# Feed-forward of a streaming encoder: weights of two projections prepared once for both token sets, the third projection accumulated whole in PSUM

## The chip, the cores and the metric

The kernel runs on one core of a Trainium2 chip. The metric is device time in microseconds (us), the lower the better. Five engines work side by side, each through a list of instructions in a fixed order: PE (matrix products; its weight loads, PEld, overlap them), DVE and POOL (elementwise work; DVE reads PSUM too), ACT (copies, casts, activation functions; reads PSUM too) and SP, which here only issues DMA transfers. An instruction waits until what it needs is there, and all behind it on its engine wait with it. PSUM, where PE writes, has eight banks of 128 partitions x 512 numbers of 32 bits.

## The reference, cut to what matters

One encoder layer runs over 1088 tokens: 1024 of a prompt and 64 of a second group, all with the same weights. Projections, sparse attention, pooling and cross-attention come first; the change touches only what follows the merge. `x` is 1088 x 1024, `w_out` 1024 x 1024, `w_gate` and `w_up` 1024 x 2816, `w_down` 2816 x 1024, all in 32-bit floats:

```python
x = x + mixed @ w_out
h = x * rsqrt(mean(x * x, axis=-1) + 1e-6) * g_ffn
y = x + (silu(h @ w_gate) * (h @ w_up)) @ w_down
```

## The kernel before, in words

Activations lie transposed, features on partitions, tokens along the free dimension. The tokens are cut in two sets, `SETS = [(0, 512), (512, 576)]`.

**Three passes.** PE works on rounded numbers (type fp32r). Each operand is therefore split into a rounded part `hi` (a cast) and the rest `lo = x - hi` (a subtraction on DVE, `lo_of`, L86), and a product is three matmuls: hi*hi, hi*lo, lo*hi (`matmul3`, L120). `wblock` fetches 512 KB of weights by a DMA and splits them: the cast (`round_hi`) goes in turn to ACT (L94) and POOL (L96), the rest to DVE (L86).

**Projection by w_out** (`out_proj`, L1003 on). For each set and each of eight output blocks `f`: a `wblock`, 24 matmuls for each 512 or 288 tokens, a DVE addition into the resident `y` (L1014), a square on ACT (L1019), a sum of squares on POOL (L1020). From the sums `norm_stat` and `norm_rows` make the factor of each token, `rb`.

**Feed-forward.** The 22 blocks of 128 hidden features are taken as eleven pairs `p` (block `p` and block `p + 11`). A pair's product h @ w is seen as a 2 x 2 block product: two halves of the 1024 features, two halves of a set's tokens, two hidden blocks. It is done with seven products of sums of blocks in place of eight plain ones (Strassen's scheme). On the token side the sums are made once a set: `block_sums` (L1051 on) multiplies `y` by the norm (L1068), forms sums (L1076), casts (L1078) and subtracts (L86), for four feature blocks `k`. On the weight side `pair_product` (L1090 on) does it for each pair and set: two 512 KB loads, five sums of 128x512 (L1107, on DVE and POOL), seven casts on ACT (L1112), seven rests on DVE (`al`), 12 matmuls a product, copies of the first four results (L1119) and the additions that put the four quadrants together (L1121 to L1133, on POOL and DVE). `hidden` calls it for `w_gate` and `w_up`, applies Silu, multiplies, and splits the result `u` in hi and lo.

**Product with w_down** (`down`, L1153 on). A pair's `u` is multiplied by its rows of `w_down` in eight units, each a few matmuls and an addition into `y` (L1168). The units of a pair are run between the products of the next pair (`units`), so each output block is added to `y` eleven times.

The loops go over set 0 with pairs 0 to 10, then set 1 with pairs 0 to 10; the sums of set 1 are made in the last pair of set 0, from buffers of their own (`tg`, `st`). A scheduler sets the order of instructions on each engine from the program's order and its own estimate of durations; buffers rotate (`bufs=`), and a tile waits until the earlier user of its memory is done. All transfers named here go through SP's one list, in order.

Of the kernel before, what the change touches and what calls it, by code (L numbers as in the profile page):

```python
# [45 lines left out]
def encoder_step(ctx: ExitStack, tc: tile.TileContext, a: dict, o: list):  # L46
# [42 lines left out]
    third = [None]  # L89

    def round_hi(hi, src):
        turn[0] += 1
        if turn[0] % 2 and third[0]:
            A.copy(hi, src)  # L94
        else:
            G.tensor_scalar(hi, src, 1.0, 1.0, op0=OP.mult, op1=OP.mult)  # L96
# [873 lines left out]
    for k in range(KT):  # L970
        SP.dma_start(y[:, k], a["x_t"][k])
# [31 lines left out]
    def out_proj(i, between={}):  # L1003
        t0, n = SETS[i]
        sq = yp.tile([128, 576], F32, name="sq", tag="sq", bufs=1)
        for f in range(KT):
# [3 lines left out]
            for c0, cn in ([(t0, n)] if n <= 512 else halves(i)):  # L1010
# [40 lines left out]
    def block_sums(i, rb):  # L1051
        t0, n = SETS[i]
        h = n // 2
        hi, lo = [[hp.tile([128, 4, 288], F32R, name=f"{nm}{q}", tag=f"{nm}{q}", bufs=1) for q in range(7)]
                  for nm in ("hi", "lo")]
        for k in range(4):
            if i:
                hb = fu.tile([128, 2, 576], F32, name="tg", tag="tg", bufs=2)
                hb = [hb[:, e] for e in range(2)]
                sums = fu.tile([128, 4, 288], F32, name="st", tag="st", bufs=2)  # L1060
                sums = [sums[:, e, :h] for e in range(4)]
            else:
# [136 lines left out]
    while units:  # L1199
        units.pop(0)()  # L1200
# [65 lines left out]
```

## Time and profile before

| what | us |
|---|---|
| median of three runs (1804.94 to 1807.34) | 1806.07 |
| the profiled execution, its own time | 1805.8 |
| its span, first to last instruction | 1803.9 |
| first matmul of the projection by `w_out` | 925.2 |
| first matmul of the feed-forward | 1032.3 |
| last matmul begins | 1800.8 |

The page gives, for each engine, busy time, its share of the span and the number of instructions. A view by stretches ("windows") gives for a stretch of the span: its length, the busy time of PE, PEld, DVE, ACT and POOL each with the number of instructions in parentheses, the mean clock granted to PE (1.00 is full), the share of time that the 16 DMA engines were busy, and GB/s. A view by tiles gives for a group of instructions min/median/max of their durations in ns, and the start of the first and the last. A line of the timeline gives start, duration, engine, line, operation, output tile <- input tiles, form, and in brackets the idle time before it with what ended it. Matmuls are pipelined: one's recorded duration is longer than its distance to the next, so what PE really needs for one is read from the distances of starts.

### The profile page before, as it was taken

What the parts mean: (1) busy time and instruction counts of PE and PEld (TensorE: products, weight loads), DVE (VectorE), ACT (ScalarE), POOL (GpSimd) and SP (SyncE); (2) the same over time, 40 slices, a digit from 0 to 9 for tenths busy, and PEclk for the clock granted to TensorE, in tenths of its full rate; (3) what the DMA queues carried; (4) which work ended last, traced back from release to release, by engine and by line L of the source; (5) the groups of instructions that cost most, each with busy time, mean ns of one, the idle gap of its engine ahead of it and who ended that gap; (6) DMA issues with size and microseconds to landing.
All of it is one profiled execution on the core that took longest, in us unless ns stands there. A gap on an engine that the chain in (4) does not pass through costs nothing.

```text
span 1803.9 us, 32261 instructions
## 1 busy us (share of the span) xinstructions
PE 1731.5 (96%) x11762; PEld 1648.2 (91%) x11762; DVE 1441.2 (80%) x2779; ACT 854.4 (47%) x2013; POOL 812.7 (45%) x784
## 2 busy tenths in 40 slices
PE   6999999999999998999999899999997899999999
PEld 6999999999999998877899889899996799999999
DVE  6667999998953445889764899898899999898896
ACT  4456677726423443588422353443443434344442
POOL 4111323243531225764114665666658665555543
PEclk9999999999999999999999899999998899999999
DMA  7122441134355236721532223332322332222322
GB/s 227 60 66 83 159 137 53 57 121 131 104 165 170 86 104 235 218 90 40 220 119 84 82 88 100 103 109 82 109 91 82 105 106 91 86 95 81 106 74 73
DMA packets 123598, 198.24 MB, mean 110 GB/s; under 512 B 21031, under 2 KB 91807, under 8 KB 123438
## 3 DMA queue, kind: packets, MB, share of 16 engines
q1 hardware_dynamic: 123438, 196.16, 34.0%
q8 instruction: 93, 1.52, 0.3%
q14 instruction: 67, 0.55, 0.1%
HBM read 158.47 MB, written 37.65 MB: 109 GB/s over the span
## 4 chain that ended last, share of the span: by engine, by line
PE 58%; DVE 7%; issue 3%; POOL 2%; ACT 2%; DMA 1%; SPq 0%; DVEq 0%; ACTq 0%; POOLq 0%
PE mm L120 45%; PE fl L120 8%; PE acc L921 1%; DVE lo L86 1%; PE tr L891 1%; DVE al L86 1%; PE mm L914 1%; DVE wlo L86 1%; DMA gt<-side_m 0%; POOL ws L1107 0%; ACT pr L897 0%; PE mm L603 0%; DVE pr L895 0%; DVE ws L1107 0%; ACT ah L1112 0%
## 5 line engine op out<-in xcount | busy, mean ns | idle before, releaser
L120 PE MATMUL mm<-hi,ah 128*128 128x256 f32 (+1 forms) x1232 | 358.4, 291 | 9.9 <-ACT hi L1078 6.1
L120 PE MATMUL mm<-hi,al 128*128 128x256 f32 (+1 forms) x1232 | 358.4, 292 | 7.6 <-DVE al L86 7.6
L120 PE MATMUL mm<-lo,ah 128*128 128x256 f32 (+1 forms) x1232 | 358.9, 291 | 5.0 <-DVE lo L86 5.0
L86 DVE TENSOR_TENSOR al<-ws,ah 128x512 fp32r<-128x512 f32 x220 | 218.7, 1006 | 53.8 <-ACT ah L1112 51.5
L120 PE MATMUL mm<-u,whi 128*128 128x288 f32 (+1 forms) x1056 | 258.1, 330 | 0.7 <-DVE u L86 0.7
L1112 ACT CAST ah<-ws 128x512 fp32r<-128x512 f32 x220 | 135.4, 619 | 248.5 <-POOL ws L1107 142.0
L120 PEld LDWEIGHTS mm<-hi,ah 128*128 128x128 f32 x1232 | 234.9, 191 | 17.2 <-ACT hi L1078 8.3
L120 PEld LDWEIGHTS mm<-hi,al 128*128 128x128 f32 x1232 | 233.6, 190 | 11.9 <-DVE al L86 11.2
L120 PEld LDWEIGHTS mm<-lo,ah 128*128 128x128 f32 x1232 | 234.2, 190 | 10.9 <-DVE lo L86 6.5
L120 PE MATMUL fl<-hh,whi 128*128 128x362 f32 (+1 forms) x576 | 190.2, 331 | 1.0 <-ACT hh L133 1.0
L120 PE MATMUL fl<-hl,whi 128*128 128x362 f32 (+1 forms) x576 | 191.0, 332 | 0.0
L120 PE MATMUL fl<-hh,wlo 128*128 128x362 f32 (+1 forms) x576 | 189.8, 330 | 0.0
L120 PEld LDWEIGHTS mm<-u,whi 128*128 128x128 f32 x1056 | 175.2, 189 | 9.3 <-DVE u L86 1.1
L120 PE MATMUL mm<-u,wlo 128*128 128x288 f32 (+1 forms) x528 | 174.1, 330 | 0.0
L1107 POOL TENSOR_TENSOR ws<-raw 128x512 f32<-128x512 f32 x66 | 88.4, 1350 | 116.8 <-DVE al L86 116.8
L1168 DVE TENSOR_TENSOR y<-mm,y 128x288 f32<-128x288 f32 (+1 forms) x264 | 135.1, 525 | 7.2 <-PE mm L120 7.2
L96 POOL TENSOR_SCALAR whi<-raw 128x1024 fp32r<-128x1024 f32 x44 | 55.6, 1264 | 175.9 <-PE mm L120 160.6
L120 PE MATMUL mm<-tmhi,hh 128*128 128x256 f32 (+3 forms) x432 | 122.4, 287 | 2.1 <-POOL tmhi L96 1.1
L120 PE MATMUL mm<-tmlo,hh 128*128 128x256 f32 (+3 forms) x432 | 122.3, 286 | 0.7 <-DVE tmlo L86 0.7
L120 PE MATMUL mm<-tmhi,hl 128*128 128x256 f32 (+3 forms) x432 | 122.2, 285 | 0.0
L86 DVE TENSOR_TENSOR wlo<-raw,whi 128x1024 fp32r<-128x1024 f32 x76 | 106.7, 1403 | 14.6 <-ACT whi L94 7.3
L765 ACT ACTIVATE junk_a<-score,cand_a,sgn_a 128x512 f16<-128x512 f32 (+2 forms) x93 | 95.5, 1027 | 46.7 <-DVE cand_a L782 22.8
(372 smaller groups left out, 4767.8 us busy)
## 6 DMA issues: line engine op xcount, KB each, us to landing
raw<-in_w_up_dram SPq DMA_DIRECT2D x44, 512.0 KB, 4.2
fr<-in_w_gate_dram SPq DMA_DIRECT2D x44, 512.0 KB, 4.2
raw<-in_w_down_dram SPq DMA_DIRECT2D x44, 512.0 KB, 4.5
fraw<-in_w_gates_dram SPq DMA_DIRECT2D x24, 512.0 KB, 3.8
side<-side_a SPq DMA_DIRECT2D x8, 1088.0 KB, 6.1
raw<-in_w_out_dram SPq DMA_DIRECT2D x16, 512.0 KB, 3.7
gt<-side_m SPq DMA_DIRECT2D x16, 384.0 KB, 4.5
raw<-in_w_om_dram SPq DMA_DIRECT2D x12, 512.0 KB, 5.0
```

Of the source, the lines that this page charges most:

```text
L86: V.tensor_tensor(lo, src, hi.bitcast(F32), op=OP.subtract)
L96: G.tensor_scalar(hi, src, 1.0, 1.0, op0=OP.mult, op1=OP.mult)
L120: PE.matmul(ps, l, r, start=i == 0, stop=i == n - 1)
L765: A.activation(junk[:n, :nk], sc, AF.Sign, bias=bj, scale=1.0 if scale is None else scale[:n, j:j + 1], accum_out=sj)
L891: PE.matmul(lg[:n, i * 512:i * 512 + cn], qT[:, h, :n], kT[:, kv, s, k0 + c:k0 + c + cn], start=s == 0, stop=s == 1)
L914: PE.transpose(pt[:cn, i * n:(i + 1) * n], probs[i][:, c:c + cn], ident[:n, :n])
L921: PE.matmul(acc, vv, r, start=ji == 0 and i == 0, stop=ji == nj - 1 and i == 1)
L1107: (V if m in (0, 5) else G).tensor_tensor(t, w, part(*z), op=op)
L1112: A.copy(wf, w)
L1168: V.tensor_tensor(y[:, f, c0:c0 + cn], ps, y[:, f, c0:c0 + cn], op=OP.add)
```

## The change

The feed-forward is put in two phases, with the hidden activations `u` kept in device memory between them.

- `out_proj` writes each finished block of `y` to a new array `y_d` in device memory as well. `y` is now two tiles, one a set, and the one of set 0 is given up after the projection.
- The scheme of seven products is another one (Winograd's form): four sums of weights, four sums of tokens, and three chains of products that add up in PSUM, so that fewer results are added outside. `product` makes the split weights of a product once and runs its matmuls for every set in `sets`.
- For pairs 2 to 10, `hidden(p, (0, 1))` takes both sets at once. Pairs 0 and 1 are done early for set 0 by `direct`, with eight plain products (no sums of weights), while the token sums of set 1 are made (`second_sums`); then `hidden(0, (1,))` and `hidden(1, (1,))` do these pairs for set 1.
- `u` is written to `u_d` instead of being split at once.
- Second phase: for three chunks of 364, 362 and 362 tokens, eight banks of PSUM hold the whole output; over 22 hidden blocks `kb`, a block of `w_down` and a block of `u` are fetched and split, and each of eight banks gets three matmuls. At a chunk's end the eight banks are added to `y` (fetched back from `y_d` into twelve buffers `yt`) and written out. The weights of `w_down` are prepared three times, once a chunk.
- After the projection by `w_out` (`third[0] = 2`) all weight casts go to ACT; of the four token sums of a block one goes to POOL, of the four weight sums of a pair one.
- On the host `w_down` is laid out so that a block is read in rows of 4 KB.

```diff
     for k in range(KT):
-        SP.dma_start(y[:, k], a["x_t"][k])
+        for i, (t0, n) in enumerate(SETS):
+            SP.dma_start(ys[i][:, k], a["x_t"][k][:, t0:t0 + n])
...
                 gate_block(wo, mixed[i][0][:, :, d0:d1], mixed[i][1][:, :, d0:d1], ps)
-                V.tensor_tensor(y[:, f, c0:c1], ps, y[:, f, c0:c1], op=OP.add)
+                V.tensor_tensor(y[:, f, d0:d1], ps, y[:, f, d0:d1], op=OP.add)
+                SP.dma_start(y_d[f, :, c0:c1], y[:, f, d0:d1])
...
+    def block_sums(i, k, rb, H, sums, b12_hl=None):
+        hb = [fa.tile([128, 1024], F32, name="fr", tag="fr", bufs=2) for e in range(2)]
+        for e in range(2):
+            kk = k + 4 * e
+            V.scalar_tensor_tensor(hb[e][:, :n], ys[i][:, kk], gffn_c[:, kk:kk + 1], rb[:, :n], op0=OP.mult, op1=OP.mult)
...
+        for q, x, z, op, y_ in ((0, b11, None, None, None), (4, t1, b12, OP.subtract, b11), (2, b22, None, None, None),
+                                (5, t2, b22, OP.subtract, t1), (6, t3, b22, OP.subtract, b12),
+                                (1, b21, None, None, None), (3, t4, b21, OP.subtract, t2)):
+            if op:
+                (G if q == 6 else V).tensor_tensor(x, z, y_, op=op)
+            A.copy(H[0][q][:, k], x)
+            lo_of(H[1][q][:, k], x, H[0][q][:, k])
...
+    def pair_product(name, p, sets, outs, finish):
+            raw = fa.tile([128, 1024], F32, name="fr", tag="fr", bufs=2) if name == "w_gate" else raw_tile()
+            SP.dma_start(raw.rearrange("p (k j) -> p k j", k=KT), a[name][p + e * NP])
...
+        def product(dst, w, q, start, stop, then):
+            if turn2[0] % 2 == 0:
+                pair_w[:] = split_tiles()
+            c = slice(512 * (turn2[0] % 2), 512 * (turn2[0] % 2) + 512)
...
+            A.copy(wh, w)
+            lo_of(wlo, w, wh)
...
+            for i in sets:
+                for k in range(4):
+                    for l, r in ((wh[:, k], x), (wh[:, k], z), (wlo[:, k], x)):
+                        PE.matmul(dst[i], l, r, start=start and j == 0, stop=stop and j == 11, skip_group_check=True)
+                then(i)
...
+        product(chain, a11, 0, True, False, lambda i: A.copy(t11[i], chain[i]))
+        s1 = wsum(V, a21, OP.add, a22)
+        product(side, s1, 4, True, False, lambda i: A.copy(t22[i], side[i]))
+        s2 = wsum(V, s1, OP.subtract, a11)
+        product(chain, s2, 5, False, False, lambda i: A.copy(t12[i], chain[i]))
+        s4 = wsum(V, a12, OP.subtract, s2)
+        product(side, s4, 2, False, True, add(t12, side))
+        s3 = wsum(G, a11, OP.subtract, a21)
+        product(chain, s3, 6, False, False, add(t22, chain))
+        product(one, a12, 1, True, True, add(t11, one))
+        product(chain, a22, 3, False, True, lambda i: finish(i, t21[i], chain[i]))
...
+    EARLY = 2
+    for p in range(EARLY):
+        direct(p)
+        if p == 0:
+            rb = norm_rows(1, *st.pop())
+        for k in (2 * p, 2 * p + 1):
+            second_sums(k, rb)
...
+    for p in range(EARLY):
+        hidden(p, (1,))
+    for p in range(EARLY, NP):
+        hidden(p, (0, 1))
...
+    for c0, cn in CH:
+        acc = [mm()[:, :cn] for f in range(KT)]
+        for kb in range(NF):
+            p, e = kb // 2, kb % 2
+            first_kb = c0 == 0 and kb < 2
+            up_, nb = (dn, 2) if first_kb else (late, 4)
+            uf = up_.tile([128, 364], F32, name="uf", tag="uf", bufs=nb)[:, :cn]
+            SP.dma_start(uf, u_d[p][e, :, c0:c0 + cn])
+            wh, wlo = wblock(a["w_down"][kb], (KT, 128), *(() if first_kb else (
+                late.tile([128, 1024], F32, name="raw2", tag="raw2", bufs=4),
+                [late.tile([128, 1024], F32R, name=nm, tag=nm, bufs=4) for nm in ("wh2", "wl2")])))
...
+            A.copy(uh, uf)
+            lo_of(ul, uf, uh)
+            for f in range(KT):
+                for j, (l, r) in enumerate(((wh[:, f], uh), (wh[:, f], ul), (wlo[:, f], uh))):
+                    PE.matmul(acc[f], l, r, start=kb == 0 and j == 0, stop=kb == NF - 1 and j == 2)
+        for f in range(KT):
+            yt = late.tile([128, 364], F32, name="yt", tag="yt", bufs=12)[:, :cn]
+            SP.dma_start(yt, y_d[f, :, c0:c0 + cn])
+            V.tensor_tensor(yt, acc[f], yt, op=OP.add)
+            SP.dma_start(o[0][f, :, c0:c0 + cn], yt)
```

How instructions now stand, at the three places that the prediction speaks of. The line numbers are those of the changed program.

**SP, where the seven-product pairs take over.** Before, around the change from set 0 to set 1 (`fr` and `raw`: the two buffers for gate weights and the three for others):

```order
L110 DMA raw_16504<-in_w_down_dram 128x4x256
L1095 DMA fr_16421<-in_w_gate_dram 128x1024
L1095 DMA fr_16423<-in_w_gate_dram 128x1024
L1095 DMA raw_16602<-in_w_up_dram 128x1024
L1095 DMA raw_16604<-in_w_up_dram 128x1024
```

Now, from `direct(1)` (its result is `tg_12583`) to the first pair of set 1 (gate weights `fr_12879`, `fr_12881`):

```order
L1162 DMA u1_11270<-tg_12583 128x512
L1254 DMA uf_17540<-u0_11269 128x364
L1254 DMA uf_17576<-u0_11269 128x364
L1162 DMA u1_11270<-tg_12583 128x512
L1091 DMA fr_12879<-in_w_gate_dram 128x1024
L1091 DMA fr_12881<-in_w_gate_dram 128x1024
```

Before, nothing but weight loads stood around the gate weights' loads. Now they stand behind the store of the second half of `direct(1)`'s result and behind two loads of `u` into memory that the tile `y` of set 1 held; and they go into the two buffers `fr` that the token sums use.

**DVE, at the same place.** `fr_12849` is the second operand of the last token sums (k = 3); `lo1` to `lo6` are the rests of set 1's token sums:

```order
L1160 TENSOR_TENSOR tg_12583<-mm_12791,tg_12583 128x256
L86 TENSOR_TENSOR lo4_12280<-ws_12844,hi4_12273 128x288
L1078 TENSOR_TENSOR ws_12845<-fr_12849,ws_12844 128x288
L86 TENSOR_TENSOR lo2_12278<-fr_12849,hi2_12271 128x288
L86 TENSOR_TENSOR lo1_12277<-fr_12849,hi1_12270 128x288
L86 TENSOR_TENSOR lo6_12282<-ws_12846,hi6_12275 128x288
L1078 TENSOR_TENSOR ws_12847<-fr_12849,ws_12845 128x288
L86 TENSOR_TENSOR lo5_12281<-ws_12845,hi5_12274 128x288
L86 TENSOR_TENSOR ul_17549<-uf_17540,uh_17548 128x364
L86 TENSOR_TENSOR ul_17585<-uf_17576,uh_17584 128x364
L86 TENSOR_TENSOR lo3_12279<-ws_12847,hi3_12272 128x288
L86 TENSOR_TENSOR wlo_12887<-fr_12879,whi_12886 128x512
```

The last multiplication of `direct(1)` (first row) is followed by nine operations for the token sums and two for the second phase; only then come the rests of the first weights of the pair (last row).

**PE, from the last pair to the second phase.** Before, a product's matmuls and the units of `w_down` took turns (`hi5`: token sums of set 0; `u`: hidden activations):

```order
L120 MATMUL mm_12566<-hi5_11695,al_12563 128x256
L120 MATMUL mm_12585<-u_12487,whi_12580 128x512
L120 MATMUL mm_12585<-u_12487,wlo_12581 128x512
L120 MATMUL mm_12614<-u_12487,whi_12580 128x512
```

Now (`mm_17301`: the last chain of the last pair, set 1; `mm_17532`, `mm_17533`: the first two of the eight banks):

```order
L1115 MATMUL mm_17301<-lo3_12279,whi_17458 128x288
L1115 MATMUL mm_17301<-hi3_12272,wlo_17459 128x288
L1263 MATMUL mm_17532<-uh_17548,whi_17543 128x364
L1263 MATMUL mm_17532<-ul_17549,whi_17543 128x364
L1263 MATMUL mm_17532<-uh_17548,wlo_17544 128x364
L1263 MATMUL mm_17533<-uh_17548,whi_17543 128x364
L1263 MATMUL mm_17533<-ul_17549,whi_17543 128x364
L1263 MATMUL mm_17533<-uh_17548,wlo_17544 128x364
```

The units are gone from between the products. All 1584 matmuls by `w_down` come in one block at the end, three to a bank, with the banks in turn.

More of the change, by code (lines that the diff above doesn't have):

```diff
@@ L88, in encoder_step @@
     turn = [0]
-    third = [None]
+    third = [0]
     def round_hi(hi, src):
         turn[0] += 1
-        if turn[0] % 2 and third[0]:
+        if third[0] and (turn[0] % 2 or third[0] > 1):
             A.copy(hi, src)
@@ L1086, in encoder_step, with combos @@
-    PRODUCTS = ((0, (1, 0), OP.add, (1, 1)), (2, (0, 0), OP.add, (1, 1)), (3, (1, 1), None, None),
-                (5, (0, 0), None, None), (4, (0, 1), OP.subtract, (1, 1)), (1, (0, 0), OP.add, (0, 1)),
-                (6, (1, 0), OP.subtract, (0, 0)))
-    def pair_product(name, p, i, H, out, units, q0):
-        h = SETS[i][1] // 2
+    def combos(pool, i):
+        h = SETS[i][1] // 2
+        return [[pool.tile([128, 4, h], F32R, name=f"{nm}{q}") for q in range(7)] for nm in ("hi", "lo")]
@@ new lines, in banks, with add @@
+        def banks():
+            return {i: mm()[:, :SETS[i][1] // 2] for i in sets}
+        t11 = {i: outs[i][:, 0, 0] for i in sets}
+        t12 = {i: outs[i][:, 0, 1] for i in sets}
+        t21 = {i: outs[i][:, 1, 0] for i in sets}
+        t22 = {i: outs[i][:, 1, 1] for i in sets}
+        chain, side, one = banks(), banks(), banks()
+        def add(t, ps):
+            return lambda i: V.tensor_tensor(t[i], ps[i], t[i], op=OP.add)
+        product(chain, a11, 0, True, False, lambda i: A.copy(t11[i], chain[i]))
@@ L1181, in encoder_step @@
+    st.append(norm_stat(1, sq1))
+    y0_c.__exit__(None, None, None)
     mix_c[0].__exit__(None, None, None)
-    fu = ctx.enter_context(tc.tile_pool(name="fu", bufs=1, side="right"))
-    units = []
-    for i in range(2):
-        for p in range(NP):
-            now, later = (units, []) if p < NP - 1 else (units[:5], units[5:])
-            us = hidden(p, i, H[i], now)
-            units = now + later
-            if i == 0 and p == NP - 1:
-                H.append(block_sums(1, rb))
-            while units:
-                units.pop(0)()
-            if i == 0 and p == 1:
-                st.append(norm_stat(1, sq1))
-            if i == 0 and p == 2:
-                rb = norm_rows(1, *st.pop())
-            units = down(p, us, i)
@@ L1199, in encoder_step, with second_sums @@
-    while units:
-        units.pop(0)()
+    hp1_c = tc.tile_pool(name="h1", bufs=1)
+    HH.append(combos(hp1_c.__enter__(), 1))
+    third[0] = 2
+    fu_c = tc.tile_pool(name="fu0", bufs=1, side="right")
+    fu = fu_c.__enter__()
+    def second_sums(k, rb):
+        block_sums(1, k, rb, HH[1], [fa.tile([128, 512], F32, name="ws", tag="ws", bufs=4) for e in range(4)])
+    EARLY = 2
[5 more added lines that the diff above has]
+            second_sums(k, rb)
```

213 lines of the change are left out of this document (100 added, 113 removed).

## The prediction

> **What bounds the kernel now.** The page first, then the view by stretches, cut where the feed-forward (from 1030.4, the end of the projection by `w_out`) changes its character.
>
> ```profile
> PE 1731.5 (96%) x11762; PEld 1648.2 (91%) x11762; DVE 1441.2 (80%) x2779; ACT 854.4 (47%) x2013; POOL 812.7 (45%) x784
> ```
> ```profile
> 930.00:1030.40 100.40, 96.45 (x573) 88.01 (x571) 58.99 (x83) 29.61 (x59) 51.82 (x44) 0.97 0.30 88
> 1030.40:1382.00 351.60, 342.24 (x2357) 315.57 (x2357) 323.38 (x442) 153.15 (x299) 223.69 (x176) 1.00 0.30 98
> 1382.00:1412.00 30.00, 16.25 (x45) 11.16 (x45) 28.55 (x38) 10.63 (x25) 21.95 (x20) 0.54 0.09 27
> 1412.00:1800.80 388.80, 388.77 (x2902) 386.86 (x2900) 340.60 (x527) 153.54 (x280) 201.88 (x163) 1.00 0.29 93
> 1800.80:1803.90 3.10, 0.00 (x0) 0.00 (x0) 0.46 (x1) 0.00 (x0) 0.00 (x0) 1.00 0.33 113
> ```
>
> PE sets the time. In set 1 (1412 to 1800.8) it never idles, though DVE is busy 340.6 of 388.8 us; in set 0 (1030.4 to 1382) it idles 351.60 - 342.24 = 9.4 us. Between them, where set 1's token sums are made, it works 16.25 of 30 us, at a clock of 0.54. The view of waits says for what:
>
> ```profile
> PE mm L120 <- ACT hi L1078: 6.1, 5, 2.6
> PE mm L120 <- DVE lo L86: 5.0, 4, 1.8
> PE mm L120 <- DVE al L86: 2.7, 1, 2.7
> ```
>
> Token sums and weights come late. So weight preparation saved on DVE, ACT and POOL is worth only what PE waits for it now. What PE itself needs for a matmul is read from the distance of starts:
>
> ```profile
> 1113.53 0.28 PE L120 MATMUL mm<-hi,ah 128*128 128x256 f32 x1
> ...
> 1114.96 0.63 PE L120 MATMUL mm<-u,whi 128*128 128x512 f32 x2
> 1115.43 0.39 PE L120 MATMUL mm<-u,wlo 128*128 128x512 f32 x1
> 1115.66 0.63 PE L120 MATMUL mm<-u,whi 128*128 128x512 f32 x2
> ```
> ```profile
> 1499.78 0.30 PE L120 MATMUL mm<-hi,ah 128*128 128x288 f32 x1
> ...
> 1502.97 0.43 PE L120 MATMUL mm<-u,whi 128*128 128x288 f32 x2
> ```
> ```profile
> 299.69 0.33 PE L120 MATMUL mm<-hh,uhi 128*128 128x362 f32 x1
> ...
> 303.02 0.33 PE L120 MATMUL mm<-hh,ulo 128*128 128x362 f32 x1
> ```
>
> Twelve of 256 columns take 1.43 us (119.2 ns each), three of 512 0.70 (233.3), 24 of 288 3.19 (132.9), 20 of 362 3.33 (166.5).
>
> **The change part by part.** *Matmuls.* Before: 11 pairs x 168 = 1848 of 256 and of 288, 1848 x 252.1 ns = 465.9 us; by `w_down` 528 of 512 (123.2) and 1056 of 288 (140.3): 729.4 us. Now: `direct` 2 x 192 of 256 (45.8), the same pairs for set 1 2 x 168 of 288 (44.7), nine pairs for both sets 1512 x 252.1 (381.2), by `w_down` 1584 of about 362 (263.7): 735.4. PE's own work **grows by 6.0 us**.
>
> *What is lost now.* From 1030.4 to 1800.8 are 770.4 us; less 729.4 are **41.0 us lost**: the 9.4, at the change of sets the 13.75 idle and some 7.5 of half clock (16.25 x 0.46), the rest in hesitations shorter than the view shows, since a matmul's recorded end lies 0.16 us behind its successor's start. The places of all these go with the change. The question is what comes in their stead.
>
> *Where the pairs take over.* The tile view, min/median/max in ns:
>
> ```profile
> L86 DVE TENSOR_TENSOR al<-ws,ah x220: 676/1056/1826, 1032.3 to 1775.9; 128x512 fp32r<-128x512 f32 x110
> L86 DVE TENSOR_TENSOR al<-raw,ah x44: 677/680/1297, 1047.1 to 1769.6; 128x512 fp32r<-128x512 f32 x44
> L1107 POOL TENSOR_TENSOR ws<-raw x66: 1267/1297/1744, 1043.4 to 1772.2; 128x512 f32<-128x512 f32 x66
> L1112 ACT CAST ah<-ws x220: 600/621/632, 1031.6 to 1775.2; 128x512 fp32r<-128x512 f32 x110
> L86 DVE TENSOR_TENSOR wlo<-raw,whi x76: 1206/1225/2023, 665.4 to 1789.1; 128x1024 fp32r<-128x1024 f32 x76
> L86 DVE TENSOR_TENSOR lo<-st,hi x12: 445/826/1546, 1372.1 to 1410.1; 128x288 fp32r<-128x288 f32 x12
> L1068 DVE SCALAR_TENSOR_TENSOR tg<-y,gffn_c,rb x8: 805/1050/1349, 1353.4 to 1399.4; 128x576 f32<-128x576 f32 x8
> L1076 DVE TENSOR_TENSOR st<-tg x4: 444/1049/1049, 1367.3 to 1405.5; 128x288 f32<-128x288 f32 x4
> L1128 DVE TENSOR_TENSOR tg<-mm,tg x22: 409/433/446, 1043.5 to 1763.6; 128x256 f32<-128x256 f32 x11, 128x288 f32<-128x288 f32 x11
> ```
>
> The same DVE subtraction takes 0.68 us, or over 1 us, the latter mostly while POOL forms sums; what reads PSUM (last row) does not stretch. With one sum in four left on POOL, I take minima and add a little, and keep the medians as upper bounds. The Trainium skill ("SBUF — State Buffer", "Who interferes with whom") has the rule: a DVE instruction with two SBUF inputs and a GpSimd one that reads SBUF shut each other out. The trace agrees (0.68 against 1.06 us); by that rule alone minima would hold wherever POOL rests.
>
> Let t be the end of the projection. PE runs `direct(0)` to t + 22.9, then the small matmuls for `rb`, then `direct(1)`, to t + 46.8. From t + 24 DVE has set 1's token sums: 8 x 0.805 + 12 x 0.444 + 28 x 0.446 = 24.3, and between them two weight rests (2 x 1.21), four multiplications (4 x 0.41) and two rests of `u` (1.0): 29.3 at the minima, 53 with the medians; I take 32. The last use of `fr_12849` is some 3 us before the end: t + 53. Only then may SP load `fr_12881` into that buffer, and this and the load before it also stand behind the store of `direct(1)`. The load's price, the time SP takes to issue one, and (for below) a cast of 128x1024:
>
> ```profile
> fr<-in_w_gate_dram SPq DMA_DIRECT2D x44, 512.0 KB, 4.2
> raw<-in_w_down_dram SPq DMA_DIRECT2D x44, 512.0 KB, 4.5
> ```
> ```profile
> L1095 SPq DMA_DIRECT2D fr<-in_w_gate_dram x44: 328/341/1373, 1021.6 to 1725.7; - x44
> ```
> ```profile
> L94 ACT CAST whi<-raw 128x1024 fp32r<-128x1024 f32 x11 | 11.6, 1055 | 2.5 <-PE mm L120 2.5
> ```
>
> 4.2 us, then a sum 0.68 and a cast 0.62: the second product starts at about t + 59, when PE should have been 12.2 us into the pair and has done one product (1.6). **Lost: 10.6.** The clock adds to it:
>
> ```profile
> 1003.70:1005.80 2.10, 0.16 (x2) 0.00 (x0) 1.97 (x3) 0.41 (x2) 0.68 (x1) 1.00 0.00 0
> 1005.80:1009.20 3.40, 3.35 (x14) 3.35 (x15) 3.40 (x6) 2.35 (x6) 2.66 (x4) 0.50 0.47 154
> ```
>
> After 2.1 us of idling PE ran 3.4 us at half clock, which is 1.7 lost. With one such spell: **12 in all**. Lower bound 6 (the load waits for the store alone: a multiplication 0.4, an issue 0.34, 4.2 and 1.3), upper 33 (DVE at its medians, 21 later). The Trainium skill ("TensorE: Matmul & The Clock Gate", Part 1) halves the clock after an idle window of about 3.4 us; here 2.1 us were enough, so the measurement decides. By either the 8 us at this place are paid.
>
> *Pairs 0 and 1 for set 1.* PE 22.3 us a pair; DVE 14 x 0.68 + 6 x 0.68 + 6 x 0.44 + 1.7 = 17.9 at minima, 27 at medians. Between 0 and 10 lost; nearer the minima, since POOL has two sums of 1.3 us a pair: **2**.
>
> *Both sets.* PE 42.3 us a pair, DVE 14 x 0.68 + 6 x 0.68 + 12 x 0.43 + 3.2 = 22, at medians 31; ACT 14 x 0.62 and copies. The quoted set 1, at 88% of DVE, lost nothing; set 0, at 92%, lost 9.4. At 52 to 73%: **2** (0 to 9).
>
> *Product by w_down.* For each of 66 blocks PE has 24 x 166.5 = 4.0 us. DVE: 1.21 + 0.5; ACT: under 1.6; POOL nothing. Transfers: 524 KB of weights and 186 KB of `u` in 4.0 us, 178 GB/s, against this stretch:
>
> ```profile
> 880.00:890.00 10.00, 10.00 (x81) 10.00 (x80) 7.59 (x21) 3.35 (x7) 0.00 (x0) 1.00 1.01 409
> ```
>
> At its start two blocks (8.0 us of PE) come from older buffers; the third is loaded when the last product has ended: 4.5 + 1.05 + 1.21 = 6.8 and SP's issues, about 0.7: just hidden, and 6.8 us dear if the first two did not cover it. At a chunk's end DVE's eight additions (about 0.5 each) keep up with PE's 0.5 a bank; were they not covered, 4 us a chunk. Lost: **2** (0 to 10). The tail, last matmul to end, stays at 3.1.
>
> *Projection.* Twenty-four more stores, off PE's path. Now it loses 3.95 idle and 3% of clock, 7 in all, for DVE's sake. Set 0's token sums move twelve additions from POOL to DVE and bring four more rests; DVE at minima then has 36 us for 38 of PE in blocks 2 to 7, while POOL disturbs it less. **-1** (-4 to +4).
>
> *Sum.* Before: 1030.4 + 729.4 + 41.0 + 3.1 = 1803.9, and 1.9 around the span (own time 1805.8, 0.3 under the median of 1806.07). Now: 1029.4 + 735.4 + (12 + 2 + 2 + 2) + 3.1 = 1785.9, and 1.9: **1788**, 1.0% less.
>
> **The rivals.** (1) *The gap stays small*: DVE is done early and only the store holds the loads. For it: minima. Against: SP's order. 12 becomes 6, and the singles lose nothing: **1779**.
>
> (2) *The old stall in a new place.* Token sums at DVE's medians and a clock that stays low while PE works in bits, as from 1382 to 1412. 12 becomes 28: **1804**, no change. For it: that row. Against: POOL had 21.95 us of work in those 30, and will have four sums.
>
> (3) *Slower: transfers in the second phase.* One SP list holds loads of weights and `u`, stores, and loads of `y`, each waiting in turn. PE waits from the point at which 710 KB take over 4.0 us; the gain of 18 is used up at 0.27 us a block, so below 166 GB/s. At the 154 of the stretch quoted above: 0.6 x 66 = 40, **1828**. For it: the stretches of the feed-forward ran at 93 to 98. Against: those were asked for no more, and 409 was reached.
>
> (4) *The clock drops in the second phase.* Changing bank every 0.5 us could leave small gaps; half clock for a tenth of 264 us costs 13 to 26, **1808**. Against: set 1 changed banks as well, at 1.00. The Trainium skill (the same page, "A second HAM failure mode: psum-queue depth-cycling") reports such a kernel; no run here shows it.
>
> (5) *The preparation saved is not felt*: already the forecast, as the gain comes from the waits.
>
> **How the numbers follow.** Forecast 0.62 (own range 1782 to 1797), (1) 0.12, (2) 0.15, (3) 0.07, (4) 0.02, others 0.02. The range 1778 to 1803 holds the forecast, most of (1) and half of (2). A measurement can tell 0.2%, 3.6 us, from no change. Faster: 0.62 + 0.12 + 0.08 of (2) = 0.82; same 0.09, the rest of (2) and a little; slower 0.09 from (3), (4) and others.
>
> **What would show it.** Right: one gap of PE of 6 to 10 us about 47 us after the projection, ended by DMA of `fr` and DVE, with a clock below 1 behind it; pairs for both sets 42 to 43 us apart; 88 to 89 us for a chunk; DVE's 128x512 rests near 0.7 us. Wrong: idle PE inside the pairs for both sets, waits of PE for `raw2` or `wl2`, chunks over 90 us, or no gap at all.

## The result, and the profile after

The changed kernel takes **1780.74 us** (median of four runs, 1776.42 to 1783.87), the kernel before 1806.7 on the same chip (1804.94 to 1812.04): a ratio of 0.985, 95% interval 0.982 to 0.988. Forecast were 1788 and a range of 1778 to 1803. The gain is 26 us where 18 were forecast.

The profiled execution took 1782.27 us, with a span of 1780.5. Where the time went, by the starts of the first and last matmul of each stage:

| stage | before, us | after, us | forecast of the difference |
|---|---|---|---|
| all ahead of the projection by `w_out` (no edit reaches PE's work there) | 925.2 | 928.0 | 0 |
| projection by `w_out`, first to last matmul | 104.9 | 100.2 | -1 |
| from there to the last matmul (feed-forward) | 770.4 | 748.3 | -17 |
| last matmul's start to the end | 3.4 | 4.0 | 0 |

The first row is not the change's: in the fourteen traces of this study the projection starts anywhere from 918.5 to 928.0 us, and the program ahead of it multiplies the same in all. So stages are compared below, and times by their ratio to the kernel before on the same chip, which took 1801.8 to 1806.7 us in the several jobs. Stages alone give -4.7 - 22.1 + 0.6 = -26.2, as the medians do.

The page of the changed kernel, first part:

```profile
PE 1721.8 (97%) x11810; PEld 1672.4 (94%) x11810; DVE 1127.0 (63%) x2411; ACT 816.4 (46%) x1927; POOL 403.3 (23%) x444
```

DVE lost 314 us of work and POOL 409; PE's share still is nearly everything. The view by stretches, cut at the stages (projection; early pairs; gap; its sequel; pairs 0 and 1 for set 1; pairs for both sets; product by `w_down`; tail):

```profile
928.00:1028.40 100.40, 98.16 (x594) 88.88 (x592) 61.70 (x100) 31.26 (x66) 43.07 (x33) 1.00 0.38 121
1028.40:1077.60 49.20, 48.55 (x405) 48.35 (x404) 30.14 (x59) 20.61 (x42) 9.83 (x6) 1.00 0.34 108
1077.60:1086.00 8.40, 0.11 (x2) 0.01 (x1) 5.70 (x15) 3.79 (x9) 0.85 (x1) 0.64 0.62 200
1086.00:1089.40 3.40, 3.40 (x13) 3.18 (x14) 3.37 (x4) 0.96 (x2) 1.73 (x1) 0.50 0.00 0
1089.40:1134.40 45.00, 43.90 (x325) 43.43 (x324) 34.30 (x59) 22.61 (x46) 6.70 (x4) 0.99 0.35 114
1134.40:1515.80 381.40, 381.40 (x3027) 381.40 (x3026) 184.73 (x338) 135.76 (x287) 28.42 (x17) 1.00 0.21 72
1515.80:1776.80 261.00, 261.00 (x1585) 260.75 (x1584) 119.20 (x153) 93.91 (x129) 0.00 (x0) 1.00 0.63 208
1776.80:1780.50 3.70, 0.04 (x1) 0.00 (x0) 0.61 (x2) 0.00 (x0) 0.00 (x0) 0.89 0.63 224
```

For 642 us, from 1134.4 on, PE does not idle once. What is lost stands in three lines, the whole of the view of waits for PE from 1028 to 1780:

```profile
PE mm L1115 <- ACT whi L1107: 8.3, 1, 8.3
PE mm L1115 <- DVE tu L1129: 1.1, 2, 0.6
PE mm L1037 <- POOL sq L1029: 0.6, 1, 0.6
```

The first is the gap that was forecast at this place. Behind it PE runs 4.2 us at half clock: 3.4 in the row with 0.50, the rest in the row after it. The timeline of PE, SP, DVE and ACT there, and the longest wait in SP's list from 1074 to 1084, tell what the gap hangs on:

```profile
1078.75 0.41 DVE L1160 TENSOR_TENSOR tg<-mm,tg 128x256 f32<-128x256 f32 x1
1079.45 0.43 SPq L1162 DMA_DIRECT2D u<-tg  x1
1079.98 0.38 SPq L1091 DMA_DIRECT2D fr<-in_w_gate_dram  x1
1081.20 0.44 DVE L1078 TENSOR_TENSOR ws<-fr,ws 128x288 f32<-128x288 f32 x1
1081.70 0.33 SPq L1091 DMA_DIRECT2D fr<-in_w_gate_dram  x1
1085.32 0.62 ACT L1107 CAST whi<-fr 128x512 fp32r<-128x512 f32 x1 [3.00 <-DMA fr<-in_w_gate_dram]
1085.99 0.61 PE L1115 MATMUL mm<-hi,whi 128*128 128x288 f32 x1 [8.29 <-ACT whi L1107]
```
```profile
SPq L1254 <- DVE fr L1071: 4.0, 1, 4.0
```

SP's list stands still for 4.0 us until DVE's last multiplication by the norm (L1071), which is done at 1078.46: the two loads of `u` (L1254) go into memory that `y` of set 1 held, and it reads `y`. The store of `direct(1)` goes out behind them (1079.45), the first load of gate weights right behind the store (1079.98). The last multiplication of `direct(1)`, too, waits its turn among the token sums on DVE (1078.75, though PE began its last matmul at 1077.43), but its result is there at 1079.16, before SP comes to the store. The first load lands 5.2 us after its issue, where the median of these loads is 3.6. The second load waits for the last token sum that reads its buffer (1081.20 to 1081.64) and is issued at 1081.70; PE does not wait for that one. In the pairs that follow DVE's rests take their minimum, where their median was 1.06 us before:

```profile
L86 DVE TENSOR_TENSOR wlo<-ws,whi x88: 677/687/694, 1088.9 to 1499.0; 128x512 fp32r<-128x512 f32 x88
```

### The profile page after: what moved, and what is told of

Read it like the earlier page. It is cut to its first block, busy times and chain, and to the rows that moved or that the text cites. A ratio compares the mean times of both kernels' runs of the same rounds, so it can differ in the third digit from the quotient of the medians.

```text
span 1780.5 us, 31511 instructions
## 1 busy us (share of the span) xinstructions
PE 1721.8 (97%) x11810; PEld 1672.4 (94%) x11810; DVE 1127.0 (63%) x2411; ACT 816.4 (46%) x1927; POOL 403.3 (23%) x444
## 4 chain that ended last, share of the span: by engine, by line
PE 61%; DVE 6%; DMA 2%; issue 1%; POOL 1%; ACT 1%; SPq 0%; DVEq 0%; ACTq 0%; POOLq 0%
PE mm L1115 24%; PE mm L1263 14%; PE mm L120 11%; PE fl L120 7%; PE acc L921 1%; PE tr L891 1%; DVE lo L86 1%; PE mm L914 1%; DVE wlo L86 1%; DVE fr L1071 1%; DMA side_a<-gt 1%; DVE ws L1078 0%; PE mm L603 0%; DVE pr L895 0%; DVE pl L86 0%
## 5 line engine op out<-in xcount | busy, mean ns | idle before, releaser
L1115 PE MATMUL mm<-hi,whi 128*128 128x288 f32 (+1 forms) x1120 | 324.0, 289 | 9.4 <-ACT whi L1107 8.3
L1115 PE MATMUL mm<-hi,wlo 128*128 128x288 f32 (+1 forms) x1120 | 324.9, 291 | 0.0
L1115 PE MATMUL mm<-lo,whi 128*128 128x288 f32 (+1 forms) x1120 | 324.2, 290 | 0.0
L1115 PEld LDWEIGHTS mm<-hi,whi 128*128 128x128 f32 x1120 | 212.6, 190 | 10.1 <-ACT whi L1107 8.5
L1115 PEld LDWEIGHTS mm<-lo,whi 128*128 128x128 f32 x1120 | 212.5, 190 | 0.0
L1115 PEld LDWEIGHTS mm<-hi,wlo 128*128 128x128 f32 x1120 | 211.9, 189 | 0.2 <-DVE wlo L86 0.2
L1263 PE MATMUL mm<-uh,wh 128*128 128x362 f32 (+1 forms) x512 | 167.4, 328 | 0.0
L1263 PE MATMUL mm<-ul,wh 128*128 128x362 f32 (+1 forms) x512 | 166.8, 326 | 0.0
L1263 PE MATMUL mm<-uh,wl 128*128 128x362 f32 (+1 forms) x512 | 166.0, 326 | 0.0
L120 PEld LDWEIGHTS fl<-hh,wlo 128*128 128x128 f32 x576 | 108.5, 188 | 0.6
```

The lines of the kernel that those rows point to most:

```text
L120: PE.matmul(ps, l, r, start=i == 0, stop=i == n - 1)
L1115: PE.matmul(dst[i], l, r, start=start and j == 0, stop=stop and j == 11, skip_group_check=True)
L1263: PE.matmul(acc[f], l, r, start=kb == 0 and j == 0, stop=kb == NF - 1 and j == 2)
```

## The experiments

All edits are of the changed kernel, and every kernel computes the whole layer. "FF" is the time from the projection's last matmul to the last matmul of all, in the run's trace (changed kernel: 748.3); "ratio" is to the kernel before on the same chip.

| run | median, us | ratio, 95% interval | projection | FF |
|---|---|---|---|---|
| the changed kernel | 1780.7 | 0.985 (0.982 to 0.988) | 100.2 | 748.3 |
| e1 buffers exchanged | 1774.0 | 0.984 (0.983 to 0.986) | 100.2 | 746.8 |
| e2 factor early | 1770.6 | 0.982 (0.981 to 0.984) | 100.2 | 740.2 |
| e3 both | 1767.8 | 0.981 (0.980 to 0.983) | 100.2 | 740.3 |
| e4 no early pairs | 1792.3 | 0.995 (0.993 to 0.997) | 100.2 | 763.2 |
| e5 preparation twice | 1779.7 | 0.986 (0.983 to 0.988) | 100.2 | 748.2 |
| e6 sets apart | 1801.4 | 0.997 (0.996 to 0.999) | 100.2 | 771.2 |
| e7 two late buffers | 1779.7 | 0.986 (0.984 to 0.989) | 100.2 | 750.4 |
| e8 four buffers for y | 1783.5 | 0.989 (0.986 to 0.992) | 100.2 | 748.8 |
| e9 sums twice too | 1776.6 | 0.986 (0.984 to 0.987) | 100.2 | 748.6 |
| e10 set 1's sums on POOL | 1777.5 | 0.986 (0.985 to 0.988) | 100.2 | 748.8 |
| e11 moved by 32 bytes | 1766.7 | 0.980 (0.979 to 0.982) | 100.4 | 740.2 |
| e12 set 0's sums on POOL | 1782.4 | 0.987 (0.984 to 0.990) | 103.2 | 747.8 |

### What the gap hangs on: e1, e2, e3

e1 changes which buffers pair 0 of set 1 uses:

```diff
-raw = fa.tile(..., name="fr", tag="fr", bufs=2) if name == "w_gate" else raw_tile()
+raw = fa.tile(..., name="fr", tag="fr", bufs=2) if (name == "w_gate") == (p > 0) else raw_tile()
```

> For pair 0 of set 1 the gate weights go into the buffers that otherwise take the up weights (free, and loaded, before the projection's early pairs end), and the up weights into the two buffers of the token sums. Theory A (the token sums of set 1, late on DVE, hold the first product: first by the buffers and then by their own rests, which end 5.7 us after the last matmul of the early pairs): the gap of 8.3 us turns into several short waits of 3 to 5 us in all, and the time falls by 3 to 8 us against the changed kernel's 1780.7, to about 1775. Rival B (only the load behind the store holds PE): the gap goes wholly, with its half clock 10.3 us, to about 1770.5. Rival C (something else holds PE, for instance the small matmuls or PSUM banks): no change.

The first product now starts at once, and the wait stands ahead of the second, 5.25 us long:

```profile
1069.47 0.29 PE L1115 MATMUL mm<-hi,wlo 128*128 128x288 f32 x1
1075.01 0.61 PE L1115 MATMUL mm<-hi,whi 128*128 128x288 f32 x1 [5.25 <-ACT whi L1107]
```
```profile
1075.00:1078.50 3.50, 3.47 (x13) 3.12 (x14) 3.28 (x6) 1.24 (x2) 2.87 (x1) 0.50 0.41 157
```

DVE and ACT in that time:

```profile
1072.63 0.68 DVE L1098 TENSOR_TENSOR ws<-raw 128x512 f32<-128x512 f32 x1
1075.10 0.44 DVE L86 TENSOR_TENSOR lo<-ws,hi 128x288 fp32r<-128x288 f32 x1
1073.71 0.40 ACT L1131 COPY tg<-mm 128x288 f32<-128x288 f32 x1 [0.68 <-DMA u<-tg]
1074.34 0.62 ACT L1107 CAST whi<-ws 128x512 fp32r<-128x512 f32 x1
```

The weight sum for the second product (1072.63) stands among the token sums on DVE, whose last rest is done at 1075.5, and its cast (1074.34) behind an ACT copy that waits 0.7 us for the store of `direct(1)`, and behind a cast of the token sums. The row of the windows shows the half clock after it. So the wait moved, and FF fell by 1.5 us only, less than the 3 to 8 of theory A and far from rival B's 10: with the loads free, most of the wait is for DVE, which still has token sums to make; about 1 us, from the end of the weight sum to its cast, is for what stands ahead on ACT.

e2 makes the factor `rb` earlier; the rest of DVE's work follows from it:

```diff
         for name in ("w_gate", "w_up"):
+            if between and name == "w_up":
+                between()
...
-        direct(p)
-        if p == 0:
-            rb = norm_rows(1, *st.pop())
+        direct(p, (lambda: rbs.append(norm_rows(1, *st.pop()))) if p == 0 else None)
+        rb = rbs[0]
```

> The small matmuls that make the factor rb of set 1 stand between the gate and the up product of the first early pair, 11.5 us earlier; nothing else is edited (the scheduler then also puts the loads of gate weights ahead of the last stores). Theory A: DVE's token sums start some 11 us earlier and end before the early pairs do, so the gap of 8.3 us and its half clock go: 9 to 11 us less than 1780.7, about 1770.5. Rival B: the same, since the loads stand ahead of the stores now. A rival to both (DVE has too much in the early pairs, sums and rests of weights compete and the early pairs now wait for their own weights): 0 to 5 us less, the wait moved into the early pairs.

The gap is gone. What is left for PE, from the projection's end to the end of the program, is this:

```profile
PE mm L1115 <- DVE wlo L86: 1.4, 1, 1.4
PE mm L1115 <- DVE tu L1129: 1.1, 2, 0.6
PE mm L1037 <- POOL sq L1029: 0.6, 1, 0.6
PE mm L1115 <- ACT tg L1131: 0.3, 1, 0.3
```

FF is 8.1 us shorter. A and B expect the same here, as the scheduler also moved the loads ahead of the stores; but e1, where the loads were free and the sums late, won little, so it is theory A that stands: the late token sums make the gap, and they are late because they cannot start before `rb`. In the changed kernel DVE has made the tiles from which PE forms `rb` by 1037.3, but PE comes to it at 1053.4, behind all of `direct(0)`. Of the gap a wait of 1.4 us for a rest and one of 0.3 are left. e3 has both edits:

> Both edits, the factor early and the buffers exchanged for pair 0. Theory A: nothing is left to be won by the exchange once the sums are early: the same as the run with the early factor, within 2 us, about 1770. Rival B: the same. If the buffers are a bound of their own even with early sums: 3 or more us below the run with the early factor alone.

740.3 us, the same as e2 to 0.1. The buffers are no bound of their own. Against e1 the edit of e3 is the early factor alone, with the loads free in both: 6.5 us less (740.3 for 746.8), which is the plainest sign that the late sums are the cause. e3 is the fastest form of this program that was run but for e11, which measures the same.

### What the early pairs are worth: e4

```diff
-    EARLY = 2
+    EARLY = 0
+    rb = norm_rows(1, *st.pop())
+    for k in range(4):
+        second_sums(k, rb)
```

> No early pairs: all eleven pairs go through the seven-product scheme for both sets, and set 1's token sums stand between the projection and pair 0 with nothing of PE beside them. PE's own work falls by 5.8 us (768 - 672 matmuls in place of 720: 1848 x 252.1 ns = 465.9 for 471.7). Theory A: PE idles for the token sums (29 to 33 us) and the first weights (6), with about 2 us of half clock, in place of the 10.3 and 1.4 lost now: 20 to 25 us slower than 1780.7, about 1803, the time before the change. Rival D (the early pairs are not what pays; the first product can start on the first sums): up to 5 us slower only, about 1784.

```profile
1054.43 0.58 PE L1115 MATMUL mm<-hi,whi 128*128 128x256 f32 x1 [27.12 <-ACT whi L1107]
```
```profile
1020.00:1054.40 34.40, 4.13 (x23) 3.54 (x21) 23.21 (x55) 12.77 (x32) 11.67 (x7) 0.56 0.11 35
```

FF is 14.9 us longer, between the two theories: the direction of A and not its size. PE idles 27.1 us and not the 35 to 39 that were added up: DVE is busy for 23.2 us of the 34.4 only. So two thirds of the feed-forward's gain hang on the two early pairs, which cost PE 5.8 us more work.

### Is it preparation, or its closeness? e5, e6, e9

e5 makes casts and rests once for each set in the pairs for both sets (the block that makes `wh` and `wlo` goes inside `for i in sets`):

```diff
-            wh, wlo = [t[:, c] for t in pair_w]
-            A.copy(wh, w)
-            lo_of(wlo, w, wh)
             for i in sets:
+                ...
+                wh, wlo = [t[:, c] for t in pair_w]
+                A.copy(wh, w)
+                lo_of(wlo, w, wh)
```

> In the pairs for both sets every cast and rest of weights is made once for each set, into tiles of their own, instead of once for both: 14 more casts on ACT (0.62 us each) and 14 more rests on DVE (0.68) a pair, nine pairs, so 78 us more of ACT and 86 us more of DVE; loads and sums stay. Theory A (preparation was never what PE waited for): the time from the projection's last matmul to the last matmul stays at 748.3 us of the changed kernel's trace within 3 us, although DVE goes from 48% to about 71% of these pairs. Rival E (preparation made once is felt): 8 us or more longer, a tenth of the work added.

```profile
1132.80:1514.10 381.30, 381.30 (x3026) 381.30 (x3025) 266.43 (x464) 203.74 (x413) 22.05 (x17) 1.00 0.22 72
```

DVE has 82 us more in these pairs and PE no pause. As theory A has it.

e6 takes the sharing away instead:

```diff
-    for p in range(EARLY, NP):
-        hidden(p, (0, 1))
+    for i in range(2):
+        for p in range(EARLY, NP):
+            hidden(p, (i,))
```

> Pairs 2 to 10 are run for set 0 and then for set 1, each with its own loads, sums, casts and rests, as before the change; the early pairs, the seven products in their new form and the second phase stay. So the sharing of weights between the sets is undone and nothing else. Theory A: set 1's sums still lie in the early pairs, so the old stall doesn't come back; DVE has about 17 us of work at the minima for 20.1 of PE in a pair of set 0 (85%): 0 to 6 us longer than 748.3 from the projection's last matmul to the last. Rival E: 9.4 us that set 0 lost before, or more, come back: 10 us or more longer.

FF grows by 22.9 us, about what the whole change had won there (22.0). Theory A falls at this run, rival E's number stands. The waits of PE in these pairs:

```profile
PE mm L1115 <- DVE wlo L86: 7.6, 9, 1.2
PE mm L1115 <- DVE tu L1129: 7.5, 18, 0.6
```

Two kinds, and neither is in the changed kernel's pairs for both sets. Nine times, in eight of the nine pairs of set 0, a rest of weights on DVE is late, mostly by about a microsecond. Eighteen times, once in each pair and set, PE stops inside a chain:

```profile
1194.17 0.39 PE L1115 MATMUL mm<-hi,whi 128*128 128x256 f32 x1 [0.28 <-DVE tu L1129]
...
1371.35 0.40 PE L1115 MATMUL mm<-hi,whi 128*128 128x288 f32 x1 [0.55 <-DVE tu L1129]
```

The product before and the one behind (`q` = 6 and 3) go into the same bank; the partial sum has to be read by DVE (`add(t22, chain)`) before PE may add to it. By the distances of starts this costs 0.44 us a pair of set 0 and 0.71 of set 1, together 10.4 us; the late rests cost 9.0, and the remaining 3 to 4 us are hesitations shorter than the view shows. With two sets the other set's product of 1.4 to 1.6 us lies between. The two waits of 1.1 us in all in the changed kernel are those of pairs 0 and 1, which are made for one set.

The late rests have a sign of another cause. DVE itself waits in these pairs for loads of gate weights:

```profile
DVE ws L1098 <- DMA fr<-in_w_gate_dram: 13.4, 13, 2.1
```

In each of the eight pairs DVE's longest such wait stands 5.0 us ahead of PE's wait for the late rest (DVE starts again at 1186.02, PE at 1190.99), and in seven of them PE's is shorter by 0.45 to 0.47 us (0.93 for 1.39, 1.04 for 1.50, 0.27 for 0.72). In the pairs for both sets DVE waits for no load, neither in the changed kernel nor in e9 below. So 9 of the 22.9 us follow loads that come too late when each pair's weights are fetched once for each set.

So was it the amount of work that e5 had not doubled, the sums and loads? e9 doubles the sums too:

```diff
-            t = fa.tile([128, 512], F32, name="ws", tag="ws", bufs=4)
-            eng.tensor_tensor(t, x, z, op=op)
+            for _ in sets:
+                t = fa.tile([128, 512], F32, name="ws", tag="ws", bufs=4)
+                eng.tensor_tensor(t, x, z, op=op)
```

> Pairs for both sets in which the weight sums, too, are made twice (DVE 3 x 0.68 and POOL 1.3 us more a product pair, so 6 more sums of DVE and 2 of POOL a pair), beside casts and rests made for each set. So DVE, ACT and POOL do nearly the work of pairs made for one set at a time, but PE still runs a product for one set and then for the other. What cost 23 us when the sets were run apart: Theory H (not the amount of preparation but its closeness: with one set a product follows 1.4 to 1.6 us after the last, the next weights and the reading of a chain's partial sum in PSUM must fit in that): 0 to 3 us longer than 748.3 from the projection's last matmul to the last. Rival E (the amount of work on DVE and POOL): 10 us or more longer.

```profile
1130.10:1511.40 381.30, 381.30 (x3025) 381.30 (x3025) 315.87 (x517) 200.95 (x413) 44.03 (x34) 1.00 0.23 74
```

And here is e6, set 0 and then set 1:

```profile
1130.50:1324.90 194.40, 184.58 (x1502) 180.94 (x1500) 157.68 (x256) 98.43 (x206) 30.11 (x18) 1.00 0.34 119
1324.90:1535.10 210.20, 204.96 (x1525) 202.83 (x1525) 154.43 (x263) 103.94 (x208) 28.41 (x17) 1.00 0.32 112
```

In e9 DVE has 315.9 us of work and PE never waits; in e6 DVE has 312.1 and PE idles 15. FF of e9 is 748.6. Rival E falls: it is not the amount of work on DVE and POOL. Theory H fits what is seen inside the chains, 10.4 us: sharing puts a second product between two steps that need each other. For the late rests, 9.0 us, H is not shown, because e9 makes the loads once and e6 twice (DMA at 0.23 and 0.33): there the closeness that counts may be that of loads and buffers. No run with the sets apart and more buffers for the loads was made.

### The second phase: e7, e8

```diff
-up_, nb = (dn, 2) if first_kb else (late, 4)
+up_, nb = (dn, 2) if first_kb else (late, 2)
...
-late.tile([128, 1024], F32, name="raw2", tag="raw2", bufs=4)
+late.tile([128, 1024], F32, name="raw2", tag="raw2", bufs=2)
```

(and the same for `wh2` and `wl2`)

> In the second phase two buffers in place of four for each of raw weights, their casts, their rests, u and its parts. A buffer for raw weights then turns over in 3.7 to 4.5 us of load, 1.05 of cast and 1.2 of rest, about 7 with SP's issue, for 2 x 4.0 of PE; a pair of casts and rests in 2.3 and 4.0. Theory A (transfers have room, 178 GB/s asked for, over 400 reached elsewhere): 0 to 4 us longer, most of it at the chunks' ends. Rival F (the second phase lives on its deep buffers; one list of SP with stores and loads of y between cannot keep up): a wait of 1 us or more in most of the 66 blocks, 40 us or more longer.

FF is 2.1 us longer, the tail 1.0; no wait of PE shows in the view of waits. Theory A: transfers have room. The 2.1 us are no waiting at all: the 1584 matmuls start 166.1 ns apart on average, in place of 164.7, which makes 2.1 us (the last section has more on this). The second edit is `bufs=12` to `bufs=4` for `yt`:

> Four buffers for y at a chunk's end in place of twelve. Theory A: the fifth addition waits for the store of the first (addition 0.5, issue 0.4, store 2 to 3) and then for its own load (2.5 to 3.5), some 6 us, and PE's banks with it, less what PE does in the first banks (2 us): 3 to 5 us at two chunk changes and 4 at the end, 10 to 14 us longer. Rival G (loads of y come early enough and the next chunk's first blocks hide it): only the tail grows, 0 to 5 us.

FF is 748.8, the tail 7.6 in place of 4.0. DVE waits 13.4 us for `y`, but at the chunk changes PE has banks enough and does not:

```profile
DVE yt L1267 <- DMA yt<-y_d: 13.4, 9, 3.1
```

Rival G: only the end pays, 3.6 us for the twelve buffers.

### POOL and DVE: e10, e12

```diff
-(G if q == 6 else V).tensor_tensor(x, z, y_, op=op)
+(G if q == 6 or i == 1 and q in (5, 3) else V).tensor_tensor(x, z, y_, op=op)
```

> Three of set 1's four token sums of a block on POOL, in place of one (L1078). Theory A with the step of the prediction that DVE's durations are set by POOL: DVE's subtractions stretch towards 1 us for 512 columns and 0.8 for 288 while POOL works, and each of POOL's sums takes 0.85 to 1.3 us and waits for the one before, so the token sums end 4 to 12 us later and the gap of 8.3 us grows to 12 to 20. Rival J (DVE is relieved of 8 sums of 0.37 us and ends earlier): the gap shrinks by 1 to 3 us.

The gap is 7.2 us, then PE waits 0.8 for a rest; FF is 748.8, 0.5 more. Theory A's 12 to 20 us are refuted; the gap shrinks by about 1, rival J's lower bound, but nothing is won by it. DVE's groups in the 46 us from 1040, of the changed kernel:

```profile
L86 DVE TENSOR_TENSOR lo<-ws,hi 128x288 fp32r<-128x288 f32 x16 | 7.5, 481 | 1.2 <-ACT hi L1079 1.2
L86 DVE TENSOR_TENSOR lo<-fr,hi 128x288 fp32r<-128x288 f32 x12 | 5.7, 497 | 0.0
L1078 DVE TENSOR_TENSOR ws<-fr,ws 128x288 f32<-128x288 f32 x8 | 3.6, 446 | 0.0
```

and of e10:

```profile
L86 DVE TENSOR_TENSOR lo<-ws,hi 128x288 fp32r<-128x288 f32 x16 | 9.6, 607 | 1.2 <-ACT hi L1079 1.2
L86 DVE TENSOR_TENSOR lo<-fr,hi 128x288 fp32r<-128x288 f32 x12 | 6.9, 608 | 0.4 <-ACT hi L1079 0.4
```

The stretching is there, a subtraction takes 0.61 us where it took 0.49. It costs DVE 3.3 us in these two groups, and the eight sums that POOL took from it were 3.6. They cancel.

For set 0's sums, beside the projection, the edit is the same with `i == 0`:

> Set 0's token sums, made beside the projection by w_out: three of four of a block on POOL (twelve in all, as many as before the change), in place of one; nothing else. The changed kernel's projection takes 100.2 us from first to last matmul, the one before took 104.9. Theory A (the prediction's step: POOL's reading stretches DVE's subtractions, so DVE is late for PE's weights): DVE's subtractions of 256 columns go from 0.58 to 0.8 us or more, and the projection takes 102 to 105 us. Rival M (the gain there is from elsewhere, such as the time at which set 0's sums start, or chance): 100 to 101 us.

The projection takes 103.2 us, 3.0 more: theory A's time. Groups of DVE from 915 to 1026, e12:

```profile
L86 DVE TENSOR_TENSOR lo<-fr,hi 128x256 fp32r<-128x256 f32 x12 | 10.0, 860 | 0.0
L86 DVE TENSOR_TENSOR lo<-ws,hi 128x256 fp32r<-128x256 f32 x16 | 7.2, 488 | 0.0
```

The first is at 0.86 us (0.57 in the changed kernel), the second at 0.49 (0.59), so on average the durations hardly move (0.61 for 0.56); what counts is which of them stand ahead of PE's weights. POOL works through from 1004.7 to 1010.3, and while it does every DVE instruction that reads SBUF twice is slow, the rest of the next weights, too, at 1.81 us for the 1.21 it takes alone:

```profile
1006.14 0.96 DVE L86 TENSOR_TENSOR lo<-fr,hi 128x256 fp32r<-128x256 f32 x1
1007.02 0.94 DVE L86 TENSOR_TENSOR b12l<-fr,b12h 128x256 fp32r<-128x256 f32 x1
1007.88 1.81 DVE L86 TENSOR_TENSOR wlo<-raw,whi 128x1024 fp32r<-128x1024 f32 x1
```

PE waits 2.97 us for that rest, until 1009.7, with a slow clock behind it:

```profile
1009.00:1013.00 4.00, 3.25 (x15) 3.25 (x16) 4.00 (x7) 2.04 (x5) 2.32 (x2) 0.66 0.47 165
```

### A by-product: e11

```diff
+    pad = const.tile([128, 8], F32, name="pad")
+    V.memset(pad, 0.0)
     ident_r = const.tile([128, 128], F32R, name="ident_r")
```

> The run with both edits (early factor, exchanged buffers), and a tile of 32 bytes a partition placed ahead, so that tiles in SBUF begin at multiples of 64 bytes where they began 32 bytes behind one. The trace of the changed kernel shows blocks of the second phase whose matmuls of 362 columns start 160.7 ns apart, others 166.5, in a fixed turn of four, as the four buffers take turns. Theory K (where the tile of moving numbers begins sets this): matmuls of 256 columns come nearer 113 ns than 119, of 288 nearer 127 than 133, of 362 nearer 160 than 165: 15 to 40 us less in all. Rival L (the turn comes from something else): no change, within 2 us of the run with both edits.

FF 740.2, the same; the blocks of `w_down` keep their turn of 166.5, 160.7, 164.2 and 164.7 ns. Rival L: the absolute place of tiles in steps of 64 bytes is not it.

## Why the prediction was right, and where it was off

- **The bound.** That PE sets the time and that preparation counts only where PE waits: right. The 41 us lost before became 10.5 at the gap and its sequel (8.4 and 2.1 of half clock), 3.4 in the early pairs (the small matmuls for the factor, and a wait of 0.6 for the sum of squares), 1.4 at the two chain waits, and little else.
- **The gap.** Forecast: 10.6 us, and 1.7 for the clock, ended by the load of `fr`, at t + 47. Measured: 8.4 and 2.1, at t + 49 (t = 1028.2). The step that was not right is which load binds. The text held PE at the second product for the load that waits for the last use of `fr_12849`, at t + 53; that load did go out at t + 53.5, but PE was held by the first load, behind the store and the two loads of `u` that wait for DVE's last reading of `y`, and the second came in its shadow. That the size came so near, by another load than the one that was priced, is in part luck. e1 and e2 show the cause one step earlier: the sums start late, at the factor. Rival (1), with the store alone, fails in e1. Rival (2) fails too: DVE's rests went to their minima, and the half clock lasted for one spell.
- **Pairs for both sets.** Forecast 2 us lost, measured 0 (381.4 us for 381.2). The reason given, that DVE is at 52 to 73% there, is not what decides: e9 has DVE at 83% and loses nothing, e6 has it at 77% and loses 22.9 us.
- **Rival (5)**, "the preparation saved is not felt", was folded into the forecast. The amount isn't felt (e5, e9). But the same edit takes dependent steps apart and fetches weights half as often, and undoing both costs all that FF won (e6: 10.4 us inside the chains, 9.0 behind late loads). The prediction did not have this term: it priced the new scheme's chains at nothing, and would have missed their waits in pairs made one set at a time.
- **Product by `w_down`.** Forecast 263.7 + 2 lost, measured 260.7. Nothing was lost, and a matmul of 362 columns takes 164.7 ns on average here, where the quoted row gave 166.5: 1584 x 1.8 ns = 2.9 us. Rival (3) is refuted by e7: half the buffers cost 3 us, not 40, and 2.1 of the 3 are the matmuls' pace. Rival (4): the clock was 1.00 all through.
- **Projection.** Forecast -1 (-4 to +4), measured -4.7. The mechanism was right, as e12 gives 3.0 of it back; the size was too small. Before, two waits of 1.99 and 1.29 us were each followed by 3.4 us at half clock, 3.4 us lost in all; now two waits of 1.02 and 1.16 us are followed by none. The forecast knew of 7 us lost there and gave back 1.
- **The sum.** Against the terms: projection -3.7, product by `w_down` -5.0, pairs for both sets -1.8; early pairs, gap and single pairs together +1.7 (106.2 for 104.5 us); tail +0.6. These are -8.2 us, and the median came out 7.3 under 1788. It lies below the forecast's own range of 1782 to 1797 and next to rival (1)'s 1779, so the time alone would not tell the two apart. The trace does: the gap cost 10.5 us and not 6, and the miss lies in the projection and the product by `w_down`.

## What to carry to other kernels

When a change both saves work on a helping engine and reorders the main one, price the distance between dependent steps, not the share of busy time: here nearly the same work on DVE (316 and 312 us) went with no wait of PE in e9 and with 23 us lost in e6, 10.4 of them by what lay between two steps of one chain. Where an accumulation in PSUM is read half-way, put another product between the read and the next addition. And where a stretch of work is late, look for its first operand (here a factor of a few small matmuls, worth 8 us once it was made earlier), before giving it buffers.

## What the runs showed of the hardware

- **How long an idle PE keeps its clock** is not told by the length of the wait alone. Waits of 1.45 us (e2) and 1.17 (e3) left the granted clock at 1.00; 2.97 (e12), 5.25 (e1) and 8.29 us (the changed kernel) were followed by half clock, as the 2.1 us that the prediction shows. But before the change a wait of 1.29 us in the projection was followed by 3.4 us at half clock (first two rows). And one wait of 1.8 us, some 50 us ahead of the projection (PE waits there for DVE's `ot`, L926), stands in all fourteen traces: in four, the changed kernel's among them, the clock stays at 1.00 behind it (third row), in ten it falls to 0.50 (fourth row, of e6):

```profile
1021.40:1022.70 1.30, 0.03 (x1) 0.03 (x1) 1.30 (x2) 0.41 (x1) 1.30 (x2) 1.00 0.47 25
1022.90:1026.30 3.40, 3.40 (x16) 3.40 (x16) 1.03 (x3) 0.89 (x2) 1.97 (x3) 0.50 0.78 275
879.50:883.00 3.50, 3.45 (x28) 3.48 (x29) 1.57 (x4) 0.75 (x2) 0.00 (x0) 1.00 0.96 331
874.50:877.70 3.20, 3.15 (x15) 3.18 (x16) 0.63 (x2) 0.34 (x1) 0.00 (x0) 0.50 0.94 300
```

- **Half clock comes in whole spells.** In the fourteen traces' records of the granted clock every spell, but for the one in which a program ends, lasts 3.41 us or a whole multiple (6.83; 10.24 at the changed kernel's gap, 1079.9 to 1090.2; 27.3 at the change of sets before), and within a trace all spells begin on one grid of 3.41 us. Where a wait lies on that grid may decide what it costs; no run tried this alone.
- **A matmul's price follows its buffer.** In the last two chunks blocks of 24 matmuls of 362 columns take 166.5, 160.7, 164.2 and 164.7 ns each in a fixed turn of four, and there are four buffers of each kind. With two buffers of each (e7) the turn is one of two, 165.6 and 166.1 ns. Moving most tiles by 32 bytes changes nothing (e11). What sets it stays open.
- **The same program ahead of the change** ends anywhere within 9.5 us in the fourteen traces (918.5 to 928.0). A difference of a few microseconds in this kernel is read in a stage, not in the total.
